# Gated tiles of an MLP split 70 places later, and per-token factors spread by two split-format matmuls

## The chip, the cores and the metric

The kernel runs on one core of a Trainium2 chip. A core has five engines, each with a queue of its own that it works through in order: TensorE (PE in the profile, matmuls; PEld is the loading of their weights), VectorE (DVE), ScalarE (ACT), GpSimd (POOL) and SyncE (SP, which here only issues DMAs). Engines wait for each other by semaphores. The metric is the device time of one execution in microseconds (us); less is better. Before the change it is 2059.86 us, the median of 3 runs (2059.63 to 2059.95).

## What is computed

One encoder layer on 512 tokens of 2048 channels in float32. Cut to the calls that matter:

```python
def rms_norm(x, g):
    xf = x.astype(jnp.float32)
    y = xf * lax.rsqrt(jnp.mean(xf * xf, axis=-1, keepdims=True) + EPS)
    return (y * g.astype(jnp.float32)).astype(x.dtype)
...
    xn = rms_norm(x, attn_norm_g[l])
    proj = jnp.einsum("bsd,dc->bsc", xn, w_in[l])
    u_val, u_gate, q, k, v = jnp.split(proj, split_pts, axis=-1)
    y_conv = conformer_conv(u_val, u_gate, ...)      # gate, conv of width 31, layer_norm, silu
    y_na = neighborhood_attention(heads(q), heads(k), heads(v), rpb[l])
    mixed = jnp.concatenate([rms_norm(y_conv, conv_out_g[l]), rms_norm(y_na, na_out_g[l])], axis=-1)
    x = x + jnp.einsum("bsc,cd->bsd", mixed, w_out[l])
    xn = rms_norm(x, ffn_norm_g[l])
    up = jnp.einsum("bsd,df->bsf", xn, w_up[l])
    up = depthwise_conv(up, ffn_dw_w[l], ffn_dw_b[l])      # width 3
    gate, val = jnp.split(up, 2, axis=-1)
    x = x + jnp.einsum("bsf,fd->bsd", jax.nn.silu(gate) * val, w_down[l])
return rms_norm(x, final_norm_g)
```

The inner width of the gated MLP is 5632, that is 44 tiles of 128 rows.

## The kernel before, in words

Channels lie on the 128 partitions and the 512 tokens along the free dimension, so a tile is 128x512. All large products are made from split operands: a float32 tile becomes a high part in the reduced matmul format (F32R) and a low part, the rest, in the same format. `parts` (lines 111 to 116) does this for weights: the high part `whi` by ACT, then the low part `wlo` by DVE, 128x1024 each. `mm3` (lines 122 to 127) then makes three matmuls of each pair: high by high, high by low, low by high. `whi` and `wlo` have four buffers each, the loaded weights (`raw`) seven; `weights` (lines 146 to 151) orders loads and splits three units ahead of their use.

The order of the work: the code is written as one stream, and a scheduler (the tile framework) hands each engine its instructions by a priority that counts up along the program. `shifted(by)` (lines 77 to 83) moves what stands inside it by so many places in that count. `tick` (lines 132 to 140) runs the next piece of a side job (statistics, attention) behind a matmul.

Per-token factors: a normalisation needs 1/sqrt of a mean over channels, which lie on partitions. `rsqrt_steps` (lines 170 to 198) sums squares by small matmuls with a matrix of ones, which leaves one value per token, tokens on partitions (128x4); computes the root and a Newton step on these; and then spreads the values over all 128 partitions and back onto the token axis: DVE multiplies the identity by each column of the values (`dg`, line 190, four 128x128 blocks), and one matmul with `ones` (`st`, line 193) adds up each column. With `keep`, ACT copies the result to SBUF (line 197); this is so at five uses (first norm, layer norm, both group norms, MLP norm). The last norm, in two halves, reads it from PSUM and has `keep=False`.

The MLP (lines 585 to 776) works in 11 chunks (c) of 4 inner tiles (i). For each inner tile, `up` (lines 638 to 699) makes gate and value with seven products instead of eight (a Strassen-like scheme: sums of weights `ws` and `raw` by DVE in `factors`, lines 585 to 611). A product is seven 512-column matmuls with `whi` (line 646), eight 256-column ones with `wlo` (line 651) and a last with `whi`. The first chunk uses `up_apart` with plain `mm3`. `hidden` (lines 738 to 745) scales by the MLP norm's factor, makes the width-3 convolution (`conv3`: one ACT step and two DVE steps each, the taps, lines 732 to 735), the silu (ACT, 743) and gate times value (DVE, 744). `in_two` (lines 747 to 751) splits the gated tile: `hh` by ACT (749), `hl` by DVE (750), and line 774 calls it for the four tiles at the end of a chunk. `down` (lines 753 to 765) multiplies the four split tiles of the chunk before by `w_down`, two output tiles (pd) per unit of weights: `mm3` over four tiles, a copy out of PSUM by ACT (764), and a DMA by POOL that adds it to the output in DRAM (765). Between the products of chunk c stand the down units of chunk c-1, at places 3 and 6 of the seven products (`down_units`, lines 616 to 623). The last chunk's down products come at the very end (`half`, lines 816 to 830), followed by the last norm.

Of the kernel before, what the change touches and what calls it, by code (L numbers as in the profile page):

```python
# [10 lines left out]
F32 = mybir.dt.float32  # L11
F32R = mybir.dt.float32r
AF = mybir.ActivationFunctionType
ALU = mybir.AluOpType
AX = mybir.AxisListType

P = 128
D = 2048
S = 512
# [47 lines left out]
def layer(ctx: ExitStack, tc: tile.TileContext, xT, w_in, w_out, w_up, w_down, par, tab, out):  # L67
    nc = tc.nc
    consts = ctx.enter_context(tc.tile_pool(name="consts", bufs=1))
    wpool = ctx.enter_context(tc.tile_pool(name="w", bufs=3))  # L70
    tp = ctx.enter_context(tc.tile_pool(name="t", bufs=NT))
    sm = ctx.enter_context(tc.tile_pool(name="sm", bufs=2))
    dram = ctx.enter_context(tc.tile_pool(name="dram", bufs=1, space=bass.MemoryType.DRAM))
    psm = ctx.enter_context(tc.tile_pool(name="psm", bufs=3, space=bass.MemoryType.PSUM))
    psa = ctx.enter_context(tc.tile_pool(name="psa", bufs=1, space=bass.MemoryType.PSUM))

    @contextmanager
    def shifted(by):

        at = tc.cur_priority  # L80
        tc.cur_priority = max(at + by, 0)
        yield
        tc.cur_priority = at + (tc.cur_priority - max(at + by, 0))

    def t2(name, dt=F32):
        return tp.tile([P, S], dt, tag="t2k", name=name)
# [12 lines left out]
        o = POFF[name] + i  # L99
        return prm[:, o:o + 1]  # L100

    ones = consts.tile([P, P], F32, name="ones")
    nc.vector.memset(ones, 1.0)
    ident = consts.tile([P, P], F32, name="ident")
    make_identity(nc, ident)
# [64 lines left out]
    def rsqrt_steps(accs, n, name, to=slice(0, S), keep=True):  # L170

        if not isinstance(accs, tuple):
            accs = accs,
        m = (to.stop - to.start) // P
        ps = psa.tile([P, 2, S], F32, tag="sc", name="st")[:, 0]
        for i in range(m):
            for acc in accs:
                nc.tensor.matmul(ps[:, i:i + 1], acc[:, to.start + i * P:to.start + (i + 1) * P], ones[:, 0:1],
                                 start=acc is accs[0], stop=acc is accs[-1])
        v, r, y = (sm.tile([P, S // P], F32, tag="rs" + c, name="rs" + c)[:, :m] for c in "vry")  # L180
        nc.vector.tensor_scalar(v, ps[:, :m], 1.0 / n, EPS, op0=ALU.mult, op1=ALU.add)
        nc.scalar.activation(r, v, AF.Sqrt)
        nc.vector.reciprocal(r, r)
        nc.vector.scalar_tensor_tensor(y, r, -0.5, r, op0=ALU.mult, op1=ALU.mult)
        nc.vector.tensor_mul(y, y, v)
        nc.vector.scalar_tensor_tensor(y, y, 1.5, r, op0=ALU.add, op1=ALU.mult)

        dg = t2("dg")
        for i in range(m):
            nc.vector.tensor_scalar(dg[:, i * P:(i + 1) * P], ident, y[:, i:i + 1], None, op0=ALU.mult)  # L190
        yield
        ps = psa.tile([P, 2, S], F32, tag="sc", name="st")[:, 0]
        nc.tensor.matmul(ps[:, :m * P], ones, dg[:, :m * P], start=True, stop=True)
        if not keep:
            return ps[:, :m * P]
        res = t2(name)
        nc.scalar.activation(res[:, to], ps[:, :m * P], AF.Copy)
        return res

    def rsqrt_value(g):  # L200
# [26 lines left out]
    ps = psa.tile([P, S], F32, tag="po", name="idle")  # L227
# [5 lines left out]
    for k in range(KD):  # L233
        x1.append(t2("x"))
        last = pin(nc.sync.dma_start(x1[k], xT[k]))
        h, l = t2("xh", F32R), t2("xl", F32R)
# [8 lines left out]
    for step in ORDER:  # L245
        i = next(a_ if step == "a" else q_)
# [9 lines left out]
    def stats1():  # L256
        for k in range(KD):
            sum_sq(acc1, x1[k], k == 0)
            if k % 4 == 3:
                yield  # L260
        for _ in range(STAT_AT):
            yield
        rstd.append((yield from rsqrt_steps(acc1, D, "rstd1")))
# [58 lines left out]
    def group_a():  # L322
        yield
        yield
        acc = t2("acc")
        nc.vector.tensor_add(acc, ys[0], ys[1])
        for i in range(2, NC_):
            nc.vector.tensor_add(acc, acc, ys[i])
        yield
        ps = psa.tile([P, 2, S], F32, tag="sc", name="st")[:, 0]  # L330
        nc.tensor.matmul(ps, ones, acc, start=True, stop=True)
        mu = t2("mu")
        nc.vector.tensor_scalar(mu, ps, 1.0 / CONV, None, op0=ALU.mult)
        acc = t2("acc")
        for i in range(NC_):
            nc.vector.tensor_sub(ys[i], ys[i], mu)
            sum_sq(acc, ys[i], i == 0)
        yield
        yield
        r = yield from rsqrt_steps(acc, CONV, "rln")  # L340
        acc = t2("acc")
        for i in range(NC_):
            nc.vector.tensor_mul(ys[i], ys[i], r)
            nc.scalar.activation(ys[i], ys[i], AF.Silu, scale=pc("lng", i), bias=pc("lnb", i))
            ma.append(split(ys[i], pc("cog", i), "ma"))
        for i in range(NC_):
            sum_sq(acc, ys[i], i == 0)
        for _ in range(RA_AFTER):
            yield

        ra.append((yield from rsqrt_steps(acc, CONV, "ra")))
# [123 lines left out]
    p, n = -1, 0  # L475
# [140 lines left out]
    def down_units(c, i, at):  # L616

        n = U // CH
        if not c:
            return ()  # L620
        if c < NCH - 1:
            return {3: (4 * i,), 6: (4 * i + n,)}.get(at, ())
        return {(1, 3): (0,), (1, 6): (2,), (2, 3): (4,), (2, 6): (6,), (3, 6): range(8, KD, n)}.get((i, at), ())
# [114 lines left out]
    def hidden(f, between):  # L738
        g, v = (up_apart if f < CH else up)(f, between)
        nc.vector.tensor_mul(g, g, rstd2[0])  # L740
        nc.vector.tensor_mul(v, v, rstd2[0])
        g, v = conv3(g, f), conv3(v, NF + f)
        nc.scalar.activation(g, g, AF.Silu)
        nc.vector.tensor_mul(g, g, v)
        return g

    def in_two(g):
        h, l = t2("hh", F32R), t2("hl", F32R)
        nc.scalar.activation(h, g, AF.Copy)
        nc.vector.tensor_sub(l, g, h.bitcast(F32))  # L750
        return h, l

    def down(hs, ds, wide=False):

        for d0 in ds:
            w = weights()
            for d in range(d0, d0 + U // CH):

                ps = (psm.tile([P, S], F32, tag="mm", name="pd") if wide and d % 5 > 1 else
                      psa.tile([P, S], F32, tag="tr", name="pd", bufs=2))  # L760
                for k in range(CH):
                    mm3(ps, w, (d - d0) * CH + k, *hs[k], k == 0, k == CH - 1)
                t = t2("pdc")
                nc.scalar.activation(t, ps, AF.Copy)  # L764
                nc.gpsimd.dma_start(xd[d], t, accum_op=ALU.add)  # L765

    pend = None
    for c in range(NCH):
        hs = []
        for i in range(CH):  # L770

            last = c == NCH - 1 and i == CH - 1
            hs.append(hidden(c * CH + i, lambda at: None if last else down(pend, down_units(c, i, at))))
        hs = [in_two(h) for h in hs]
        if not last:
            pend = hs

# [140 lines left out]
```

## Time and profile before

| | before |
|---|---|
| median of 3 runs | 2059.86 us |
| the profiled execution | 2060.74 us |
| its span | 2059.0 us |
| granted TensorE clock, mean | 0.997 |
| DMA, mean | 134 GB/s |

The span is the time from the first to the last instruction on the chip; the execution has 1.7 us around it. In the rows below, a line such as `L750 DVE TENSOR_TENSOR hl<-uy,hh 128x512` is line 750 of the kernel on DVE, writing tile hl from uy and hh. A timeline row begins with its start and its length in us; `x7` at its end means seven instructions merged into it, and a bracket tells how long the engine stood idle before it and what released it. Matmuls overlap: their cost is the distance from start to start, not their length. In a stretch row, busy times of the engines stand in the order PE, PEld, DVE, ACT, POOL, each with a count, and then the granted clock, the DMA share and GB/s.

### The profile page before, as it was taken

To read this page: it belongs to the slowest core of one execution; us is meant where nothing else is said; L and a number is where in the kernel's file an instruction comes from. 1 tells how busy PE (TensorE), PEld (TensorE's weight loads), DVE (VectorE), ACT (ScalarE), POOL (GpSimd) and SP (SyncE) were. 2 spreads that over 40 slices of the span, in tenths; PEclk is the share of its full clock that TensorE was granted. 3 is DMA by queue.
4 is the path that set the end of the run, shared out by engine and by line. 5 is a ranking of instruction groups with operands and counts; after the bars stand their busy time and mean duration, and the time that the engine had idled before them with its cause. 6 is when DMAs were issued, how large, how long until landed. Compare 5 with 4: busy or idle time off the path is not lost.

```text
span 2059.0 us, 28552 instructions
## 1 busy us (share of the span) xinstructions
PE 2038.8 (99%) x10810; PEld 1734.1 (84%) x10810; DVE 1665.1 (81%) x2316; ACT 1065.3 (52%) x1728; POOL 156.3 (8%) x186
## 2 busy tenths in 40 slices
PE   9999999999999999999999999999999999999997
PEld 7887888787788998888888888888888888888887
DVE  7986697687567898888888878878888888889876
ACT  6244424447436545555555555555554554555562
POOL 0000000000001001111111111111111111110110
PEclk9999999999999999999999999999999999999998
DMA  7323232335436535656566565565565566564682
GB/s 252 107 90 101 72 123 82 111 95 175 149 106 170 147 113 129 138 145 134 131 150 138 125 148 143 128 144 143 132 135 143 125 145 144 134 138 124 147 211 82
DMA packets 99113, 275.38 MB, mean 134 GB/s; under 512 B 10912, under 2 KB 15520, under 8 KB 98976
## 3 DMA queue, kind: packets, MB, share of 16 engines
q1 hardware_dynamic: 73616, 227.40, 36.6%
q0 software_dynamic: 25216, 46.15, 15.6%
q8 instruction: 85, 1.39, 0.3%
q14 instruction: 52, 0.43, 0.1%
q10 hardware_dynamic: 144, 0.01, 0.0%
HBM read 218.99 MB, written 54.53 MB: 133 GB/s over the span
## 4 chain that ended last, share of the span: by engine, by line
PE 93%; DVE 3%; DMA 1%; issue 1%; ACT 1%; SPq 0%; DVEq 0%; ACTq 0%
PE pu L646 23%; PE pu L651 12%; PE pd L127 8%; PE pd L125 8%; PE pd L126 8%; PE pj L125 7%; PE pj L126 7%; PE pj L127 7%; PE po L125 3%; PE po L126 3%; PE po L127 3%; PE pu L125 1%; PE pu L127 1%; PE pu L126 1%; DVE hl L750 1%
## 5 line engine op out<-in xcount | busy, mean ns | idle before, releaser
L115 DVE TENSOR_TENSOR wlo<-raw,whi 128x1024 fp32r<-128x1024 f32 x364 | 444.3, 1221 | 247.1 <-ACT whi L114 225.8
L114 ACT ACTIVATE whi<-raw 128x1024 fp32r<-128x1024 f32 x364 | 384.4, 1058 | 469.1 <-PE pj L126 175.3
L646 PE MATMUL pu<-xc,whi 128*128 128x512 f32 x2240 | 573.5, 392 | 0.3 <-ACT pl L658 0.3
L646 PEld LDWEIGHTS pu<-xc,whi 128*128 128x128 f32 x2240 | 408.6, 189 | 74.1 <-ACT pl L658 0.7
L651 PEld LDWEIGHTS pu<-xc,wlo 128*128 128x128 f32 x2240 | 305.6, 190 | 21.8
L651 PE MATMUL pu<-xc,wlo 128*128 128x256 f32 x2240 | 312.3, 282 | 0.0
L125 PE MATMUL pj<-xh,whi 128*128 128x512 f32 x640 | 252.4, 398 | 0.9 <-DVE gate L301 0.5
L127 PE MATMUL pd<-hh,wlo 128*128 128x512 f32 x640 | 249.1, 391 | 2.2 <-DVE wlo L115 2.2
L126 PE MATMUL pj<-xl,whi 128*128 128x512 f32 x640 | 250.2, 391 | 0.1
L125 PE MATMUL pd<-hh,whi 128*128 128x512 f32 x640 | 250.0, 391 | 0.0
L127 PE MATMUL pj<-xh,wlo 128*128 128x512 f32 x640 | 249.8, 390 | 0.0
L126 PE MATMUL pd<-hl,whi 128*128 128x512 f32 x640 | 249.1, 389 | 0.0
L765 POOL DMA_DIRECT2D x2d<-pdc x160 | 139.3, 872 | 1168.1 <-ACT pdc L764 1065.0
L658 ACT ACTIVATE pl<-pu 128x256 f32<-128x256 f32 x280 | 105.1, 380 | 173.4 <-PE pu L646 173.4
L316 DVE SCALAR_TENSOR_TENSOR y<-ch,prm,y 128x508 f32<-128x508 f32 (+14 forms) x240 | 173.1, 741 | 4.1
L114 ACT ACTIVATE whi<-ws 128x1024 fp32r<-128x1024 f32 x132 | 139.7, 1058 | 68.0 <-PE pu L646 43.5
L115 DVE TENSOR_TENSOR wlo<-ws,whi 128x1024 fp32r<-128x1024 f32 x132 | 160.9, 1219 | 1.3 <-ACT whi L114 1.2
L125 PEld LDWEIGHTS pj<-xh,whi 128*128 128x128 f32 x640 | 120.0, 188 | 32.3 <-issue 3.7
L127 PEld LDWEIGHTS pd<-hh,wlo 128*128 128x128 f32 x640 | 120.2, 188 | 30.9 <-DVE wlo L115 5.7
L764 ACT ACTIVATE pdc<-pd 128x512 f32<-128x512 f32 x160 | 93.9, 588 | 95.9 <-PE pd L127 95.9
L126 PEld LDWEIGHTS pj<-xl,whi 128*128 128x128 f32 x640 | 120.3, 188 | 26.0 <-DVE xl L238 1.8
L126 PEld LDWEIGHTS pd<-hl,whi 128*128 128x128 f32 x640 | 120.2, 188 | 25.6
(172 smaller groups left out, 2775.0 us busy)
## 6 DMA issues: line engine op xcount, KB each, us to landing
raw<-in_w_up SPq DMA_DIRECT2D x176, 512.0 KB, 3.7
raw<-in_w_down SPq DMA_DIRECT2D x88, 512.0 KB, 4.0
x2d<-pdc POOLq DMA_DIRECT2D x160, 256.0 KB, 4.8
raw<-in_w_in SPq DMA_DIRECT2D x76, 512.0 KB, 3.9
raw<-in_w_out SPq DMA_DIRECT2D x32, 512.0 KB, 3.8
x<-in_xT SPq DMA_DIRECT2D x32, 256.0 KB, 5.5
tab<-in_tab SPq DMA_DIRECT2D x32, 256.0 KB, 4.5
x2d<-x SPq DMA_DIRECT2D x16, 256.0 KB, 2.2
```

The costliest lines, as they stand in the source:

```text
L114: i = nc.scalar.activation(hi[:, :n], raw[:, :n], AF.Copy)
L115: j = nc.vector.tensor_sub(lo[:, :n], raw[:, :n], hi[:, :n].bitcast(F32))
L125: nc.tensor.matmul(ps, hi[:, a], mh, start=start, stop=False)
L126: nc.tensor.matmul(ps, hi[:, a], ml, start=False, stop=False)
L127: return nc.tensor.matmul(ps, lo[:, a], mh, start=False, stop=stop)
L316: nc.vector.scalar_tensor_tensor(y[:, a:b], h[:, a + j - PAD:b + j - PAD], prm[:, o + j:o + j + 1], y[:, a:b], op0=ALU.mult, op1=ALU.add)
L646: return nc.tensor.matmul(ps, w[0][:, k * P:(k + 1) * P], comb[c][k], start=k == 0, stop=k == U - 1)
L651: nc.tensor.matmul(ps[:, H:], w[1][:, k * P:(k + 1) * P], comb[c][k][:, :H], start=False, stop=False)
L658: nc.scalar.activation(to, ps, AF.Copy)
L750: nc.vector.tensor_sub(l, g, h.bitcast(F32))
L764: nc.scalar.activation(t, ps, AF.Copy)
L765: nc.gpsimd.dma_start(xd[d], t, accum_op=ALU.add)
```

## The change

Two edits. At the end of each chunk of the MLP but the last, the split of the four gated tiles is put 70 places further down the program's order. And where `rsqrt_steps` keeps its result, the per-token values are split into a high and a low part, two 128x512 diagonal tiles in the split format are made by one DVE product each (identity and values both spread by a stride of zero), and two accumulating matmuls in that format take the place of one in full precision. The matrix of ones becomes an F32R tile, read as float32 elsewhere.

```diff
-    ones = consts.tile([P, P], F32, name="ones")
+    ones_r = consts.tile([P, P], F32R, name="ones")
+    ones = ones_r.bitcast(F32)
...
-        dg = t2("dg")
-        for i in range(m):
-            nc.vector.tensor_scalar(dg[:, i * P:(i + 1) * P], ident, y[:, i:i + 1], None, op0=ALU.mult)
+        if not keep:
+            dg = t2("dg")
+            for i in range(m):
+                nc.vector.tensor_scalar(dg[:, i * P:(i + 1) * P], ident, y[:, i:i + 1], None, op0=ALU.mult)
+            yield
+            ps = psa.tile([P, 2, S], F32, tag="sc", name="st")[:, 0]
+            nc.tensor.matmul(ps[:, :m * P], ones, dg[:, :m * P], start=True, stop=True)
+            return ps[:, :m * P]
+
+        yh = sm.tile([P, S // P], F32R, tag="rsh", name="rsh")
+        nc.vector.tensor_copy(yh, y)
+        nc.vector.tensor_sub(y, y, yh.bitcast(F32))
+        ds = []
+        for part in (yh.bitcast(F32), y):
+            ds.append(t2("dg", F32R))
+            nc.vector.tensor_mul(ds[-1].rearrange("p (i k) -> p i k", k=P), ident.unsqueeze(1).broadcast_to([P, m, P]),
+                                 part.unsqueeze(2).broadcast_to([P, m, P]))
         yield
         ps = psa.tile([P, 2, S], F32, tag="sc", name="st")[:, 0]
-        nc.tensor.matmul(ps[:, :m * P], ones, dg[:, :m * P], start=True, stop=True)
-        if not keep:
-            return ps[:, :m * P]
+        for i, dg in enumerate(ds):
+            nc.tensor.matmul(ps, ones_r, dg, start=i == 0, stop=i == 1)
         res = t2(name)
-        nc.scalar.activation(res[:, to], ps[:, :m * P], AF.Copy)
+        nc.scalar.activation(res, ps, AF.Copy)
         return res
...
-        hs = [in_two(h) for h in hs]
+        with shifted(0 if last else 70):
+            hs = [in_two(h) for h in hs]
         if not last:
             pend = hs
```

## Prediction

> **What bounds the kernel now.** I read the page's busy line and its chain first, then the stretches, then the waits of TensorE (PE), then the timelines of PE and VectorE (DVE) where the changed code runs.
>
> ```profile
> PE 2038.8 (99%) x10810; PEld 1734.1 (84%) x10810; DVE 1665.1 (81%) x2316; ACT 1065.3 (52%) x1728; POOL 156.3 (8%) x186
> PE 93%; DVE 3%; DMA 1%; issue 1%; ACT 1%; SPq 0%; DVEq 0%; ACTq 0%
> ```
>
> PE is busy 99% of the span and is 93% of the chain that ended last. So a change can gain only by fewer PE cycles or by the few pauses of PE that are left, and it loses whatever new pause it puts into PE's queue. Four stretches (the columns are time, PE, PEld, DVE, ACT and POOL busy, then PE's granted clock):
>
> ```profile
> 520.00:580.00 60.00, 58.95 (x311) 47.31 (x312) 35.21 (x58) 28.54 (x53) 0.00 (x0) 1.00 0.36 114
> 700.00:720.00 20.00, 20.00 (x164) 19.52 (x163) 19.12 (x32) 10.51 (x14) 0.00 (x0) 1.00 0.34 104
> 960.00:1120.00 160.00, 159.73 (x845) 137.48 (x844) 133.74 (x169) 87.25 (x136) 17.42 (x20) 1.00 0.60 136
> 2045.00:2059.00 14.00, 1.27 (x3) 0.50 (x2) 6.08 (x19) 0.59 (x2) 2.78 (x4) 0.53 0.45 150
> ```
>
> In the MLP (third row) PE is covered and DVE has 16% left. The one wait there is in the list of waits (us in total, times, longest), and PE's timeline shows it in place, at the end of a chunk, where the products with the next chunk's weights meet the first down products of the last chunk:
>
> ```profile
> PE pd L127 <- DVE wlo L115: 2.2, 8, 0.3
> ```
> ```profile
> 903.08 0.40 PE L125 MATMUL pd<-hh,whi 128*128 128x512 f32 x1
> ...
> 903.77 0.40 PE L126 MATMUL pd<-hl,whi 128*128 128x512 f32 x1
> 904.44 0.50 PE L127 MATMUL pd<-hh,wlo 128*128 128x512 f32 x1 [0.27 <-DVE wlo L115]
> 904.78 0.40 PE L125 MATMUL pd<-hh,whi 128*128 128x512 f32 x1
> ...
> 905.24 1.75 PE L646 MATMUL pu<-xc,whi 128*128 128x512 f32 x7
> 906.83 1.11 PE L651 MATMUL pu<-xc,wlo 128*128 128x256 f32 x8
> ```
>
> Start to start a 512-column matmul takes 0.23 us (903.08 to 903.77 are three). From 903.77 to 904.44 are 0.67, and to 904.78 another 0.34: 0.44 of wait and 0.11 to get going again, 0.55 us, eight times by the waits. One more end of a chunk has its pause elsewhere:
>
> ```profile
> 1881.26 0.39 PE L646 MATMUL pu<-xc,whi 128*128 128x512 f32 x1
> 1882.00 1.88 PE L646 MATMUL pu<-xc,whi 128*128 128x512 f32 x7 [0.34 <-ACT pl L658]
> 1883.72 1.11 PE L651 MATMUL pu<-xc,wlo 128*128 128x256 f32 x8
> ```
>
> 0.74 instead of 0.23, then seven in 1.72 instead of 1.59 (905.24 to 906.83): 0.64. All ten ends of chunks now cost 8 x 0.55 + 0.64 = 5.0 us.
>
> **Part 1, the later split of the gated tiles.** The diff sets lines 774 to 775 (hh on ScalarE, ACT; hl on DVE) 70 places later in priority. The listing of the two built programs shows what comes of it. SP's and POOL's queues keep their order to the last DMA; DVE's, ACT's and PE's change at the ends of chunks. DVE's queue here, changed kernel below (its lines stand 1 to 14 higher), names shortened to the tiles:
>
> ```
> before: wlo, tap, ws add, tap, tap, hl0, tap, hl1, g*v, hl2, wlo(down), hl3, wlo, vv add, wlo, ws add
> after:  wlo, tap, ws add, tap, tap, wlo(down), tap, wlo, g*v, hl0, ws add, wlo, hl1, raw add, hl2, hl3, vv add
> PE before: hh0 hl0 hh0' hl0' wlo0 hh1 hl1 | next product | the rest
> PE after:  hh0 hh0' hl0 wlo0 hl0' hh1 wlo0' hh1' hl1 wlo1 hh2 hl1' wlo1' hh2' hl2 wlo2 hh3 | next product
> ```
>
> (hl0 in PE's rows is the matmul that reads hl0; a dash marks the second output tile.) So the weight split for which PE waits moves ahead of hl, and hl moves behind two weight splits; hl1 and hl2 go behind two more 1024-column steps and a third. PE's queue, in order, still meets hl0 third, before the next product that could fill the time. Durations are in DVE's timeline:
>
> ```profile
> 895.78 1.23 DVE L115 TENSOR_TENSOR wlo<-raw,whi 128x1024 fp32r<-128x1024 f32 x1 [2.13 <-ACT whi L114]
> 896.97 0.75 DVE L733 SCALAR_TENSOR_TENSOR uy<-g,prm,uy 128x511 f32<-128x511 f32 x1
> 897.64 1.22 DVE L596 TENSOR_TENSOR ws<-raw 128x1024 f32<-128x1024 f32 x1
> 898.77 0.75 DVE L734 SCALAR_TENSOR_TENSOR uy<-g,prm,uy 128x511 f32<-128x511 f32 x1
> 899.43 0.75 DVE L733 SCALAR_TENSOR_TENSOR uy<-vl,fwn,uy 128x511 f32<-128x511 f32 x1
> 900.10 0.69 DVE L750 TENSOR_TENSOR hl<-uy,hh 128x512 fp32r<-128x512 f32 x1
> ...
> 903.17 1.22 DVE L115 TENSOR_TENSOR wlo<-raw,whi 128x1024 fp32r<-128x1024 f32 x1
> 904.30 0.68 DVE L750 TENSOR_TENSOR hl<-uy,hh 128x512 fp32r<-128x512 f32 x1
> 904.90 1.22 DVE L115 TENSOR_TENSOR wlo<-ws,whi 128x1024 fp32r<-128x1024 f32 x1
> 906.04 0.68 DVE L673 TENSOR_TENSOR vv<-vv,pl 128x512 f32<-128x512 f32 x1
> ```
> ```profile
> 894.69 1.06 ACT L114 ACTIVATE whi<-raw 128x1024 fp32r<-128x1024 f32 x1 [1.90 <-PE pd L126]
> ...
> 897.55 0.62 ACT L749 ACTIVATE hh<-uy 128x512 fp32r<-128x512 f32 x1
> 898.07 1.05 ACT L114 ACTIVATE whi<-raw 128x1024 fp32r<-128x1024 f32 x1
> ...
> 900.67 1.05 ACT L114 ACTIVATE whi<-ws 128x1024 fp32r<-128x1024 f32 x1
> ...
> 903.28 1.06 ACT L114 ACTIVATE whi<-raw 128x1024 fp32r<-128x1024 f32 x1
> ```
>
> Queued back to back, DVE steps follow at 1.13 us (1024 columns), 0.66 (a tap) and 0.60 (512 columns), and a 512-column result is there 0.69 after its step starts; PE starts 0.05 after DVE ends (904.39 to 904.44). DVE's run starts at 895.78 in both kernels, because its high half waits (first ACT row) until PE releases a weight buffer. This ties DVE to PE, so the lateness does not wear off from chunk to chunk. From 900.10 in the new order: wlo and tap to 901.89; the second wlo (its high half is done at 901.72) to 903.02; g*v to 903.62; hl0 ends at 904.31. PE, which reached the down products at 903.08 and did two matmuls, wants it at 903.54 and gets it at 904.36: **wait 0.82**.
>
> Next on DVE: ws add at 904.22, wlo at 905.35 (its high half, the fourth ACT row, is done at 904.34), hl1 at 906.48, ended 907.17. From hl0 to hl1 PE has six matmuls: 904.36 + 1.38 = 905.74, and it starts at 907.22: **wait 1.48**. Then raw add at 907.08, hl2 at 908.21, ended 908.90, PE at 908.95 against 907.22 + 1.38 = 908.60: **wait 0.35**. hl3 has the next product in front of it and costs nothing. On ACT hh1 stands behind that fourth row and ends near 904.9 (0.62, the hh row); PE reaches it three matmuls after hl0, at 905.05, so ACT stays hidden by 0.1 to 0.2.
>
> SP's weight loads wait for DVE to have read a buffer, so they slip with DVE:
>
> ```profile
> raw<-in_w_up SPq DMA_DIRECT2D x176, 512.0 KB, 3.7
> ```
>
> A load lands after 3.7 us and the splits of DVE wait for ACT's high half and PE's buffers, not for it; I charge nothing, and up to 0.3 per end of a chunk if that cover is gone.
>
> The waits give 2.65, and three new starts at 0.11 make it 3.0 us. I take this at all ten ends of chunks: 10 x 3.0 = 30.0, less the 5.0 that is paid now, since the wait for wlo goes: **+25.0 us**. The first and the last have other neighbours in the listing; I put no more precision into them. Bounds: without the 0.11s, 26.5 - 5.0 = 21.5; with 0.1 more on each of the thirty waits, 28.0.
>
> **Part 2, factors in split format.** Five of the seven uses keep their result and change. One full-precision matmul goes, two split-format ones come.
>
> ```profile
> 574.53 1.02 PE L193 MATMUL st<-dg,ones 128*128 128x512 f32 x2
> 574.99 0.79 PE L125 MATMUL po<-mah,whi 128*128 128x512 f32 x1
> 575.62 0.39 PE L126 MATMUL po<-mal,whi 128*128 128x512 f32 x1
> ```
> ```profile
> 571.13 0.16 DVE L185 TENSOR_TENSOR rsy<-rsy,rsv 128x4 f32<-128x4 f32 x1
> 571.33 0.17 DVE L186 SCALAR_TENSOR_TENSOR rsy<-rsy,rsr 128x4 f32<-128x4 f32 x1
> 571.53 0.88 DVE L190 TENSOR_SCALAR dg<-ident,rsy 128x128 f32<-128x128 f32 x4
> 572.31 0.69 DVE L521 TENSOR_TENSOR oa<-po,ra 128x512 f32<-128x512 f32 x1
> ```
>
> From 574.53 to 575.62 are 1.09, of which the matmul of L125 is 0.23: 0.86 for the factor. Two of the split format take 0.46: 0.40 saved, five times 2.0. On DVE the four diagonal blocks take 0.78 (571.53 to 572.31). The new ones are two small steps of 0.20 (571.13 to 571.33) and two 128x512 products. No row shows a product with both operands spread; I bound one by a 1024-column step, 1.13, and by two of the old blocks, 0.39, and take hl's 0.60, whose size and output format are the same: 1.6, 0.8 more per use. PE meets the second matmul some matmuls after the first, so most of this is hidden by them. The fifth use (700 to 720, DVE busy 19.12 of 20) has no slack on DVE: of its 0.8 I charge 0.4 (bounds 0 and 0.8). Sum **-1.6 us** (bounds -2.0, and +2 with spread products at 1.13 each, 1.1 more per use, of which 0.8 is seen).
>
> **Sum.** 25.0 - 1.6 = +23.4. The profiled execution took 2060.74 (span 2059.0), 0.88 above the median of three; the difference goes onto the median: 2059.86 + 23.4 = **2083.3 us**.
>
> **Rivals.**
> *The wait goes and none comes* (faster). The weight split is ahead of hl now, and if hl0 still ends by 903.54 the 5.0 are gained: 2059.9 - 5.0 - 1.6 = 2053.3. It decides at 0.82 us: a DVE run that starts that much earlier than 895.78. For it: 2.13 us of idle DVE ahead of that row. Against: the same row says that the idle time ended with whi, and ACT's that whi waited for PE. Chance 0.04.
> *Only hl0 is late* (no difference). If the steps between hl0 and hl2 got done in PE's time, ten waits of 0.82 + 0.11 stand against 5.0 and 1.6: +2.7, 2062.6. Against: 1.13 + 1.13 + 0.60 is more than the 1.38 of six matmuls. Chance 0.06.
> *The clock falls as well* (slower still). The last stretch shows PE at 0.53 of its clock once it mostly waits, while 520 to 580, with 1.05 us without PE, kept 1.00. The new pauses sum to 2.65 within some 5.4 us. If each end of a chunk ran its next seven wide matmuls (905.24 to 906.83) at half clock, 1.6 us more, that is +16: 2099. Against: 520 to 580, and no single pause is above 1.5. Chance 0.06.
> The Trainium skill, "TensorE: Matmul & The Clock Gate", section "A second HAM failure mode: psum-queue depth-cycling", says that frequent short pauses between groups of matmuls can make the clock swing down and up; its section "What's actually happening" wants a whole idle window of about 3.4 us before the clock halves. By the first of them the third rival comes true, by the second the clock stays up; the row 520 to 580 agrees with the second, and no run here shows the first.
> That the shift does nothing is out: the queues listed above differ.
>
> **How the numbers follow.** The forecast has 0.84 and the range 2076 to 2090, which leaves out the rivals, 0.16 together. Its low end is Part 1 at +18 (no 0.11s, each wait 0.1 shorter) and Part 2 at -2.0: +16. Its high end is Part 1 at its bound of +28 and Part 2 at its bound of +2: +30. A measurement of this kernel tells about 0.2% (4 us) from no change. Faster 0.04 (the first rival), same 0.06 (the second), slower 0.90 (the forecast and the third).
>
> **What would show it.** In the changed profile PE's waits should name hl (line 764) at each end of a chunk, about 0.8, 1.5 and 0.35 us long, and no wlo; PE's idle time grows by 20 us or more, DVE's busy time by about 4; PEclk stays at 9s; the factor's matmuls show as pairs 0.23 apart. It is wrong if hl's waits are missing, if DVE runs its wlo before 895.78's equivalent, or if a clock below 1.0 stands in an MLP stretch.

## The result, and the profile after

The changed kernel takes **2083.92 us** (median of 5 runs, 2082.29 to 2087.02) against 2059.95 for the kernel before on the same chip (5 runs, 2059.63 to 2064.78): 1.0112 times as long, 95% interval 1.01 to 1.0124. The forecast was 2083.3, with a range of 2076 to 2090. Its profiled execution took 2085.22, its span is 2083.4, 24.4 more than before.

The page's busy line, its chain of work and the first rows of PE's waits (us in total, times, longest), after:

```profile
PE 2044.3 (98%) x10810; PEld 1735.3 (83%) x10810; DVE 1667.2 (80%) x2316; ACT 1063.6 (51%) x1728; POOL 156.5 (8%) x186
PE 89%; DVE 5%; issue 2%; DMA 2%; ACT 1%; POOL 0%; SPq 0%; DVEq 0%; POOLq 0%; ACTq 0%
```
```profile
PE pd L127 <- DVE hl L764: 18.1, 17, 2.9
PE pu L660 <- ACT whi L115: 2.3, 1, 2.3
```

PE has the same number of instructions and DVE 2.1 us more of work (1665.1 to 1667.2), but PE has idle time that was not there: the span grew by 24.4 and PE's busy time by 5.5. The list of waits names hl, line 764, as the place; wlo is gone from it. The second row is a new one that the prediction doesn't have. PE's timeline at the second end of a chunk, after (before, at 903.08, it had one pause of 0.44 there):

```profile
906.16 0.62 PE L126 MATMUL pd<-hh,whi 128*128 128x512 f32 x2
907.46 0.50 PE L127 MATMUL pd<-hl,whi 128*128 128x512 f32 x1 [0.67 <-DVE hl L764]
907.79 0.40 PE L128 MATMUL pd<-hh,wlo 128*128 128x512 f32 x1
...
908.72 0.39 PE L126 MATMUL pd<-hh,whi 128*128 128x512 f32 x1
910.33 0.50 PE L127 MATMUL pd<-hl,whi 128*128 128x512 f32 x1 [1.22 <-DVE hl L764]
...
911.59 0.40 PE L126 MATMUL pd<-hh,whi 128*128 128x512 f32 x1
912.07 0.50 PE L127 MATMUL pd<-hl,whi 128*128 128x512 f32 x1
```

Read it by starts, not by brackets: 0.23 from start to start is free running. Two hh matmuls start at 906.16 and 906.39, the hl one was due at 906.62 and starts at 907.46: 0.83 with the digits that the rows round off. 908.72 to 910.33 is 1.38 too long, 911.59 to 912.07 is 0.25 too long. Behind each pause the next distance is 0.34, 0.11 over. Together 2.78 us, the same at all eight inner ends to 0.01. DVE's timeline for the same end, after:

```profile
898.87 1.23 DVE L116 TENSOR_TENSOR wlo<-raw,whi 128x1024 fp32r<-128x1024 f32 x1 [2.13 <-ACT whi L115]
...
903.18 1.22 DVE L116 TENSOR_TENSOR wlo<-raw,whi 128x1024 fp32r<-128x1024 f32 x1
...
904.98 1.22 DVE L116 TENSOR_TENSOR wlo<-ws,whi 128x1024 fp32r<-128x1024 f32 x1
...
906.71 0.69 DVE L764 TENSOR_TENSOR hl<-uy,hh 128x512 fp32r<-128x512 f32 x1
907.31 1.22 DVE L621 TENSOR_TENSOR ws<-ws,raw 128x1024 f32<-128x1024 f32 x1
908.45 1.23 DVE L116 TENSOR_TENSOR wlo<-raw,whi 128x1024 fp32r<-128x1024 f32 x1
909.58 0.69 DVE L764 TENSOR_TENSOR hl<-uy,hh 128x512 fp32r<-128x512 f32 x1
910.18 1.23 DVE L612 TENSOR_TENSOR raw<-raw 128x1024 f32<-128x1024 f32 x1
911.32 1.30 DVE L764 TENSOR_TENSOR hl<-uy,hh 128x512 fp32r<-128x512 f32 x2
```

It is the queue of the prediction, step by step: two wlo ahead of the first hl, a sum of weights and a third wlo ahead of the second. The bracket of the first row is still 2.13, as before: DVE's run starts when PE lets go of a weight buffer, so DVE never gets ahead. It is not short of time, at 80% of the span; it is late all the same.

The first end of a chunk looks otherwise. PE's timeline there, after, and the stretches around it (time, busy of PE, PEld, DVE, ACT and POOL, granted clock, DMA share, GB/s):

```profile
779.75 0.62 PE L126 MATMUL pd<-hh,whi 128*128 128x512 f32 x2
783.33 0.79 PE L127 MATMUL pd<-hl,whi 128*128 128x512 f32 x1 [2.95 <-DVE hl L764]
783.92 0.63 PE L128 MATMUL pd<-hh,wlo 128*128 128x512 f32 x1
784.35 0.63 PE L126 MATMUL pd<-hh,whi 128*128 128x512 f32 x1
```
```profile
783.00:786.40 3.40, 3.07 (x7) 2.48 (x8) 3.40 (x5) 1.86 (x6) 0.00 (x0) 0.51 0.00 0
905.00:915.00 10.00, 8.03 (x39) 5.90 (x38) 8.22 (x11) 3.98 (x9) 0.00 (x0) 1.00 0.34 105
1905.00:1908.50 3.50, 3.13 (x10) 2.56 (x11) 3.50 (x6) 2.72 (x8) 0.00 (x0) 0.65 0.78 208
```

One pause of 3.11 us, and then matmuls 0.43 apart instead of 0.23 for about 3 us: the granted clock is 0.51 (first stretch). At an inner end, with 2.46 us of waits in three pieces, it stays at 1.00 (second stretch). What decides between the two is told in the last section. The last end, at 1902.72, has a pause of 2.42, the second row of the waits, and then the low clock too (third stretch). What ACT waits for there, in its timeline of the same profile:

```profile
1904.26 1.06 ACT L115 ACTIVATE whi<-ws 128x1024 fp32r<-128x1024 f32 x1 [2.31 <-DVE ws L621]
```

In all, over the free-running distances: 4.65 at the first end, 8 x 2.78, and 4.04 at the last. Before they were 0, 8 x 0.54 and 0.61. With PE 1.60 earlier at the first end (779.75 against 781.35) the sum is -1.6 + 4.65 + 8 x 2.24 + 3.43 = **24.4**, all of the 24.4.

### The profile page after: what moved, and what is told of

It reads as the page before. It is cut to its first block, busy times and chain, and to the rows that moved or that the text cites. A ratio compares the mean times of both kernels' runs of the same rounds, so it can differ in the third digit from the quotient of the medians.

```text
span 2083.4 us, 28559 instructions
## 1 busy us (share of the span) xinstructions
PE 2044.3 (98%) x10810; PEld 1735.3 (83%) x10810; DVE 1667.2 (80%) x2316; ACT 1063.6 (51%) x1728; POOL 156.5 (8%) x186
## 4 chain that ended last, share of the span: by engine, by line
PE 89%; DVE 5%; issue 2%; DMA 2%; ACT 1%; POOL 0%; SPq 0%; DVEq 0%; POOLq 0%; ACTq 0%
PE pu L660 22%; PE pu L665 11%; PE pd L127 7%; PE pd L128 7%; PE pd L126 7%; PE pj L126 7%; PE pj L127 7%; PE pj L128 7%; PE po L126 2%; PE po L127 2%; PE po L128 2%; DVE wlo L116 1%; PE pu L126 1%; PE pu L128 1%; PE pu L127 1%
## 5 line engine op out<-in xcount | busy, mean ns | idle before, releaser
L330 DVE SCALAR_TENSOR_TENSOR y<-ch,prm,y 128x501 f32<-128x501 f32 (+14 forms) x240 | 173.3, 743 | 4.2
L128 PEld LDWEIGHTS pj<-xh,wlo 128*128 128x128 f32 x640 | 120.2, 188 | 25.8 <-DVE wlo L236 0.8
```

The costliest lines, as they stand in the source:

```text
L128: return nc.tensor.matmul(ps, lo[:, a], mh, start=False, stop=stop)
L330: nc.vector.scalar_tensor_tensor(y[:, a:b], h[:, a + j - PAD:b + j - PAD], prm[:, o + j:o + j + 1], y[:, a:b], op0=ALU.mult, op1=ALU.add)
```

## The experiments

Theory: the time is the sum of what PE waits for hl at the ten ends, by DVE's queue; the factors give a little back. Rivals: that some of it is a lower clock, and that the factors aren't a gain. All excess times below are worked out as above, from start to start in PE's timeline of the profiled execution, pauses, restarts and slow matmuls together.

| kernel | median us (runs) | ratio to before, 95% interval | first end | each inner end | last end |
|---|---|---|---|---|---|
| before | | | 0 | 0.54 | 0.61 |
| changed | 2083.92 (5) | 1.0112, 1.01 to 1.0124 | 4.65 | 2.78 | 4.04 |
| e1 factors only | 2060.87 (11) | 1.0001, 0.9992 to 1.001 | 1.95 | 0.54 | 0.58 |
| e2 shift only | 2084.09 (4) | 1.011, 1.0096 to 1.0124 | 1.85 | 2.77 | 4.33 |
| e3 shift at inner ends | 2079.27 (4) | 1.0088, 1.0074 to 1.0102 | 2.06 | 2.77 | 0.62 |
| e4 shift of 25 | 2057.83 (11) | 0.9984, 0.9975 to 0.9993 | 1.38 | 0.18 | 0.70 |
| e5 shift of 100 | 2102.68 (4) | 1.0206, 1.019 to 1.0221 | 6.48 | 4.55 | 4.15 |
| e6 shift of -30 | 2057.87 (11) | 0.9986, 0.9978 to 0.9995 | 0.98 | 0.18 | 1.26 |
| e7 hl on GpSimd | 2107.15 (4) | 1.0227, 1.0213 to 1.0241 | 6.22 | 3.9 to 6.6 | 6.27 |
| e8 shift of 28, old factors | 2057.30 (11) | 0.9983, 0.9974 to 0.9992 | 0 | 0.07 | 0.22 |
| e9 four factors | 2058.94 (10) | 0.9993, 0.9984 to 1.0002 | | | |
| e10 four factors, shift of 28 | **2055.08** (9) | 0.9975, 0.9965 to 0.9985 | 0 | 0.08 | 0.70 |
| e11 shift of 60 | 2077.36 (4) | 1.0078, 1.0064 to 1.0092 | 6.09 | 1.63 | 4.97 |
| e12 four factors again | 2059.12 (8) | 0.9995, 0.9984 to 1.0007 | 0 | 0.54 | 0.72 |

The edits are against the changed kernel unless another is named. The kernel before took 2060.6 to 2060.9 beside these runs.

**e1, the factors alone.**

```diff
-        with shifted(0 if last else 70):
+        with shifted(0):
```


> The split of the gated tiles stays where it was; only the factors are spread by two split-format matmuls. Theory (waits for hl carry the loss, the factor edit saves PE cycles): 2058 to 2059 us, 1 to 2 us below before; no wait for hl, the waits for wlo at the ends of chunks as before. Rival (the longer VectorE work of the spread products carries part of the loss): 2063 us or more, with pauses of TensorE near 47, 466, 511, 573 or 707 us.

2060.87 against 2060.9: no difference, so the saving was missed. It is made and lost again. PE's timeline of e1 at the first end, and DVE's ahead of it:

```profile
779.31 0.62 PE L126 MATMUL pd<-hh,whi 128*128 128x512 f32 x2
781.41 0.50 PE L127 MATMUL pd<-hl,whi 128*128 128x512 f32 x1 [1.48 <-DVE hl L764]
```
```profile
773.29 0.69 DVE L754 TENSOR_TENSOR g<-g,rstd 128x512 f32<-128x512 f32 x1
775.75 1.23 DVE L610 TENSOR_TENSOR ws<-raw 128x1024 f32<-128x1024 f32 x1 [1.78 <-DMA raw<-in_w_up]
...
778.03 0.75 DVE L747 SCALAR_TENSOR_TENSOR uy<-g,prm,uy 128x511 f32<-128x511 f32 x1
```

PE comes to its down products at 779.31, two us earlier than before (781.35). But on DVE a sum of weights now stands between the scaling (L754) and the taps (L747), and it waits 1.78 us for a load. Taps and hl queue behind it; PE waits 1.64. From 903.76 on PE is where it was before (903.77).

**e2, the shift alone.** Before's kernel with the shift of 70 (the last fence of the diff above, the old `rsqrt_steps`).

> Only the split of the gated tiles moves by 70 places; the factors keep their one full-precision matmul. Theory: 2083 to 2086 us, before plus 23 to 26, with the three waits for hl of 0.8, 1.4 and 0.25 us at the ends of chunks. Rival (the edits need each other): clearly below 2080.

2084.09, and 23.2 over before, as expected; the changed kernel is 24.0 over before. So the shift is nearly all of the change, and the rival is out. The 0.8 us between the two are less than the intervals tell apart (2.5 to 3 us either way). But no gain of the factors is left beside the shift either, and the traces show where it goes: with them the first end costs 4.65 instead of 1.85.

**e3, the shift at the eight inner ends alone.**

```diff
-        with shifted(0 if last else 70):
+        with shifted(70 if 0 < c < NCH - 2 else 0):
```


> Both edits, but the shift by 70 at the eight inner ends of chunks alone; the first and the last end keep the old order. Theory (in the changed kernel the first and the last end cost more than the others, because their pauses of 3.1 and 2.4 us are followed by matmuls 0.43 us apart, at half clock): 8 x 2.2 us of net waits, less 1 to 2 of the factor edit: 2076 us, and no 512-column matmul slower than 0.24 us apart after 700 us except right after a wait. Rival (all ten ends cost the same): 2079 us.

The median is 2079.27 (2078.0 to 2081.42): by the number this is the rival's 2079 and not the theory's 2076, so the traces have to tell the two apart. The theory had counted on 1 to 2 us of the factors, which e1 doesn't have. The trace gives 8 x 2.23 = 17.8 for the inner ends over e1's time of 2060.87, which is 2078.7, and no more; its own execution is the one of 2078.0. PE's timeline of e3 at one end, and the stretch around it:

```profile
1028.17 0.50 PE L127 MATMUL pd<-hl,whi 128*128 128x512 f32 x1 [0.67 <-DVE hl L764]
...
1031.04 0.51 PE L127 MATMUL pd<-hl,whi 128*128 128x512 f32 x1 [1.21 <-DVE hl L764]
```
```profile
960.00:1120.00 160.00, 158.03 (x829) 135.29 (x829) 131.41 (x166) 87.19 (x137) 17.89 (x21) 1.00 0.57 134
```

So the inner ends are waits at full clock. The ten ends don't all cost the same: without the shift the last one costs 0.62 instead of 4.04 and the first 2.06 instead of 4.65, and no clock below 1.00 is left at either. The low clock belongs to the two outer ends.

**e4, e5, e6 and e11: other shifts**, 25, 100, -30 and 60 in the place of 70.

> Both edits, with a shift of 25 places in place of 70. In the built queue hl0, hl1 and hl2 stay ahead, and the down weights' wlo goes ahead of the last hl alone. Theory (what counts is how many 1024-column steps of VectorE stand between PE and hl): the 0.55 us waits for wlo at the eight inner ends go and no wait for hl comes: 2053 to 2056 us, below before and below e1. Rival (any later split costs): above e1.

> Both edits, shift of 100 places. In the built queue hl0 stands behind more 1024-column steps still, so that TensorE should pause once for about 3.1 us at each inner end (worked from VectorE's spacings of 1.13 and 0.60 us). Theory on the waits alone: about 3.1 + 0.35 us per end, 2091 us. With the rule seen at the first end of the changed kernel (a pause of 3.1 us is followed by matmuls 0.43 us apart for about 1.5 us): 1 to 2 us more at each end, 2100 to 2110 us. Rival (the loss comes from the order of TensorE's own queue, not from how late hl is): about as the changed kernel, 2084.

> Both edits, but the split of the gated tiles put 30 places ahead of its old place. In the built queue hl0 to hl2 then stand before the down weights' wlo with less between. Theory (lateness of what TensorE meets next on VectorE): the 0.55 us waits at the inner ends go, no wait for hl: 2056 to 2059 us, near the shift of 25. Rival (only a later place frees the wlo): as before or above, 2061.

> Kernel: the changed kernel with 60 places in place of 70. Theory (the time goes by where hl stands in DVE's queue, not by the number of places; with 60 one 1024-column step fewer stands ahead of hl1, so the second wait falls from 1.4 to about 0.4): pauses of 0.8, 0.4 and 0.3 us at the inner ends with 0.11 each, about 1.8 in place of 2.78, so some 8 to 10 us less than the changed kernel: 2074 to 2077. Rival (any place beyond the covered one costs the same): 2083 to 2085.

With 25 and with -30 the inner ends cost 0.18 and the kernel is faster than before, by 3.1 and 2.8 us, which is little (0.15%), but both intervals lie below 1. For e4 more was expected: the inner ends do give 8 x 0.36 = 2.9, but of the first end's 1.95 in e1 1.38 stays, and 2060.87 - 2.9 - 0.6 is 2057.4. With 60 the second wait is 0.24 instead of 1.38, as expected, since a step of 1024 columns fewer stands ahead of hl1; that saves 8 x 1.15 = 9.2 us, but longer pauses at the first and last end (3.37 and 3.30) take 2.4 of it back, and it comes out just above the expected range. Why these two are longer with 60 than with 70 was not followed up. With 100 each inner end has one pause of 3.10 and then the low clock (the first end has 4.91, the last 2.53). PE's timeline and a stretch of e5, and a single pause elsewhere in e4 with the stretch behind it:

```profile
1038.24 0.79 PE L127 MATMUL pd<-hl,whi 128*128 128x512 f32 x1 [2.94 <-DVE hl L764]
1038.83 0.63 PE L128 MATMUL pd<-hh,wlo 128*128 128x512 f32 x1
1039.26 0.63 PE L126 MATMUL pd<-hh,whi 128*128 128x512 f32 x1
```
```profile
1037.50:1041.00 3.50, 2.76 (x7) 2.18 (x8) 3.50 (x6) 1.36 (x5) 0.00 (x0) 0.55 0.54 150
```
```profile
694.93 0.39 PE L126 MATMUL pu<-xc,whi 128*128 128x256 f32 x1 [2.04 <-ACT xc L549]
```
```profile
695.00:698.00 3.00, 3.00 (x15) 3.00 (x16) 2.65 (x8) 3.00 (x9) 0.00 (x0) 0.53 0.62 152
```

In e5 an inner end costs 4.55: 3.10 of wait, and 1.45 of slow restart and slow matmuls. With the clock the time is where the theory had it. None of the four rivals came true. The time doesn't go by the number of places alone: -30 and 25 both gain, 60 costs 17 us and 100 costs 42. What counts is which steps of DVE stand ahead of hl.

**e7, hl on GpSimd**, to take the late work off DVE.

```diff
-        nc.vector.tensor_sub(l, g, h.bitcast(F32))
+        nc.gpsimd.tensor_sub(l, g, h.bitcast(F32))
```


> The changed kernel with its shift of 70, but hl is subtracted by GpSimd in place of VectorE, so no 1024-column step can stand in front of it. Theory (VectorE's queue makes hl late): the waits of 0.8, 1.4 and 0.25 us go; the last hl, which needs gate times value, is some 1.3 us late at each end: 2065 to 2072 us. Rival (TensorE's changed order, or hh on ScalarE, costs the time): 2080 us or more.

2107.15, far from what the theory expected and, by the number, on the rival's side. The waits of PE, and DVE and POOL at one end (timelines of e7):

```profile
PE pd L126 <- ACT hh L763: 12.9, 9, 2.4
PE pd L127 <- POOL hl L764: 10.2, 10, 1.1
PE pd L128 <- DVE wlo L116: 6.0, 7, 0.9
```
```profile
1413.36 1.79 DVE L748 SCALAR_TENSOR_TENSOR uy<-g,prm,uy 128x511 f32<-128x511 f32 x1
...
1416.78 2.31 DVE L116 TENSOR_TENSOR wlo<-raw,whi 128x1024 fp32r<-128x1024 f32 x1
```
```profile
1412.89 3.42 POOL L764 TENSOR_TENSOR hl<-uy,hh 128x512 fp32r<-128x512 f32 x2 [0.79 <-ACT hh L763]
```

At this end three of the four hl are in time (at 1417.67 PE starts the hh matmul and at 1417.90, with no wait, the hl one), and only the last is waited for, 1.09. But the DVE steps that start beside POOL's take 1.79 instead of 0.75 and 2.31 instead of 1.22. All of DVE's queue is later, with it wlo, the last gated tile, its hh and its hl. So the first row of the waits, for hh, doesn't speak for the rival: ACT starts the last hh at 1421.52, after 2.60 us of waiting for gate times value on DVE. What e7 was to show, that it is DVE's queue that makes hl late, it shows for three of the four tiles, and nothing for the time.

**e8, e9, e12 and e10: the parts that gain.** e8 is before's kernel with a shift of 28. e9 and e12 have no shift, and the old full-precision factor at the MLP norm only; e10 is this with the shift of 28.

```diff
-        if not keep:
+        if not keep or name == "rstd2":
             dg = t2("dg")
...
-            return ps[:, :m * P]
+            if not keep:
+                return ps[:, :m * P]
+            res = t2(name)
+            nc.scalar.activation(res, ps, AF.Copy)
+            return res
```


> The shift alone, of 28 places, with the old full-precision factor matmul. Theory: the eight waits of 0.55 us go and the first end has no wait for hl, which e1 and e4 have there with the new factors: 2056 to 2058 us, at or below e4. Rival (the new factors save what they promise): above e4 by 1.6.

> Kernel: no shift; the split-format factor at the first norm, layer norm and both group norms, the old full-precision one at the MLP norm. Theory (the MLP norm's two longer DVE steps push the taps back at the first end of a chunk, where e1's PE waited 1.5 us for hl): with the old factor there that wait stays away and what four factors save, 4 x 0.40 = 1.6 us at most, is kept: 2058.4 to 2059.8. Rival (the first end's wait comes from PE being earlier there, whatever the factor): the wait stays and the time is e1's, 2060.9.

> Kernel: e9's once more, for a look at the first end of a chunk. Theory (the old factor at the MLP norm leaves DVE's queue there as it was): PE has no wait for hl at the first end, near 780 us, the other ends cost what they cost before the change, and the time is 2058.4 to 2059.8. Rival (the wait comes from PE being earlier there): a wait of 1.0 to 1.5 us for hl near 780, and e9's gain comes from somewhere else.

> Kernel: split-format factor at four uses as in e9, and the gated tiles' split 28 places later at the first ten ends of chunks. Theory (both savings add: e8's -2.6 us from the shift and e9's -1.0 to -1.6): 2055 to 2057, at or below e8. Rival (a pause elsewhere, as e4 had at 692, takes the factors' part back): 2057.3, e8's time.

e8 came out as expected, 2057.30: no wait at its first end, and 0.07 at the inner ones. e9's one traced execution took 5249.77 us, isn't read and isn't in the table; e12 is the same kernel with a trace. PE's timeline of e12 at the first end, and DVE's ahead of it:

```profile
779.55 0.40 PE L126 MATMUL pd<-hh,whi 128*128 128x512 f32 x1
779.79 0.39 PE L127 MATMUL pd<-hl,whi 128*128 128x512 f32 x1
```
```profile
772.50 1.22 DVE L116 TENSOR_TENSOR wlo<-raw,whi 128x1024 fp32r<-128x1024 f32 x1
773.64 0.74 DVE L751 SCALAR_TENSOR_TENSOR uy<-g,prm,uy 128x511 f32<-128x511 f32 x1
```

No pause, although PE is there 1.8 us earlier than before, and the taps follow a wlo without a load in between. So the wait of e1 comes from the order that the fifth factor brings about, not from PE's being early. e12 keeps the 1.8 us to the end in its trace (span 2057.0 against 2059.0); by the medians of e9 and e12 1.5 to 1.8, within 0.2%, and both intervals reach 1. In e10 the two gains add, as far as medians tell: 5.7 against 3.4 (e8) and 1.5 to 1.8, where the intervals of e8 and e10 overlap. PE's timeline at the second end, and the MLP stretch, of e10:

```profile
904.09 0.46 PE L127 MATMUL pd<-hl,whi 128*128 128x512 f32 x1
904.38 0.40 PE L128 MATMUL pd<-hh,wlo 128*128 128x512 f32 x1
```
```profile
960.00:1120.00 160.00, 160.00 (x843) 137.69 (x842) 134.00 (x168) 86.94 (x136) 17.48 (x20) 1.00 0.58 136
```

One distance of 0.29 is all that is left of the pauses at this end: on DVE the down products' weight split now starts ahead of hl1 (899.83 and 901.57) and the next one ahead of hl2, and each hl still ends before PE comes to it. e10 takes **2055.08**, 0.9975 of the time before: the fastest of the versions run, with four of the five factors.

## Why the prediction came true

The mechanism was right, PE waits for hl because DVE's queue is late, and it carries most of the time. The sum was 0.6 us off (23.4 forecast, 24.0 by the medians, 24.4 by the traces), and that close is luck, for its parts are not all as good.

- **What bounds it, the queues, the tie of DVE to PE**: right. DVE's rows after are the forecast ones in order, its run still starts behind the 2.13 us for whi, and the excess is the same at eight ends.
- **The three waits**: forecast 0.82, 1.48 and 0.35, found 0.83, 1.38 and 0.25, with 0.11 behind each: 2.78 instead of 3.0 per inner end, 1.8 us less for eight.
- **"I take this at all ten ends"**: the weak step. The outer ends were known to have other neighbours and were still counted like the rest. In e2 the first is 1.85 and the last 4.33 instead of 3.0: 1.2 less and 1.3 more. These and the inner ends give 25.0 - 1.8 - 1.2 + 1.3 = 23.3 for Part 1, and e2 measured 23.2 over before.
- **"PEclk stays at 9s"**: right on the page, whose slices are 52 us long, and wrong in the trace: "a clock below 1.0 in an MLP stretch" stands at both outer ends, 0.51 and 0.65. So the third rival did occur, at two of ten ends, and with it a sign that the prediction itself had named as proof against it. The rival had half clock after several short pauses; here it came after single long ones, while the inner ends, which it spoke of, kept 1.00. "No single pause is above 1.5" was wrong for the outer ends, and it is no reason for the inner ones: in e7 single pauses of 1.37 and less were enough (last section). The inner ends kept their clock because their 2.46 us are spread; of the two 3.41-us windows that hold them at 906 to 912, the emptier has PE busy for 2.37.
- **The last end**: its wait isn't for hl. There the next product comes first, and its high half waits behind ACT for a sum of weights (ws, L621) that DVE now makes after two wlo. The prediction looked for no such wait, and named hl for each end.
- **Part 2**: the saving exists (PE comes to the first end 1.60 earlier, and 2.04 in e1, for 2.0 in the sum), and the factor's matmuls stand 0.23 apart as forecast. The spread products follow at 0.60, the value that was chosen between 0.39 and 1.13. The wrong step is the cost of the fifth use: 0.4 for two longer DVE steps. These cost next to nothing themselves; the order of DVE's queue behind them changed, and a step that waits for a load got ahead of the taps. That cost 1.95 in e1, and in the changed kernel 2.8 more than in e2. I charged nothing for loads, "up to 0.3 per end of a chunk if that cover is gone"; it was gone at the first end, for 1.5 to 1.8 us.
- **The signs**: PE's idle time grew by 18.9, not "by 20 us or more", for the slow matmuls count as busy; DVE's busy time by 2.1, not "by about 4".

So Part 1 came out at +23.2 instead of +25.0 and Part 2, beside it, at +0.8 instead of -1.6: misses of -1.8 and +2.4 that nearly take each other away by luck. These are differences of medians. The trace of the changed kernel by itself shows such a trade too: 1.8 less at the inner ends, 1.6 and 1.0 more at the first and the last (4.65 and 4.04 instead of 3.0).

The Trainium skill, "TensorE: Matmul & The Clock Gate", has two rules that the prediction set against each other. Its section "What's actually happening" (a whole idle window of about 3.4 us before the clock halves) agrees with the inner ends, which kept 1.00, but a pause of 2.20 us was enough in e4, and 2.42 after; here the measurement decides. For the other section, "A second HAM failure mode: psum-queue depth-cycling", e7 shows something now: three short pauses, none above 1.38, with which the clock fell at some ends (last section).

## What to carry to other kernels

Where an engine is tied to the bound engine by a buffer, a step that is put later in its queue costs the time of all that goes ahead of it, again at every turn; write out both queues up to the next wait and add. Do this for the first and last turn by themselves, for the order there differs, one long wait can cost more than three short ones, and a step that waits for a load may have come to stand in front. A small saving early on is worth only what the next waiting place lets through, so follow it to the end before it enters the sum.

## What the runs showed of the hardware

**What decides the clock.** Single pauses of up to 1.84 us (first end in e3) left the clock at full speed. Pauses of 2.20 (e4), 2.38 and 2.58 (e7), 2.42 (after), 2.53 (e5), 2.69 (e2) and of 3.1 and more came with some 3 us of matmuls at 0.43 us per 512 columns instead of 0.23, or 0.21 instead of 0.12 per 256. But the single pause isn't what decides. In e7 the inner ends from 1163 on have the same three pauses, 1.01, 1.34 and 1.37 within 6 us, and three of these six ends fell to a low clock, three did not.

The record of the granted clock in the traces shows more. Within each trace it changes only at whole multiples of 3.41 us from its first change (the end of the trace aside), and each of the 23 low stretches between 690 and 1960 us, in thirteen traces (all but e9's), lasts 3.41 or 6.83 us. So one can cut a trace into windows of 3.41 us by this grid. Here are two windows in a row at each of two ends of chunks of e7, the first pair from one that fell (the first busy time is PE's, the clock stands third from the end):

```profile
1166.59:1170.01 3.42, 1.15 (x5) 0.67 (x4) 3.42 (x3) 2.00 (x6) 1.46 (x1) 1.00 0.26 101
1170.01:1173.42 3.41, 3.41 (x12) 2.82 (x11) 2.19 (x3) 0.00 (x0) 0.00 (x0) 0.50 0.54 153
1419.18:1422.59 3.41, 2.23 (x8) 1.38 (x8) 3.41 (x5) 1.07 (x4) 0.31 (x1) 1.00 0.46 154
1422.59:1426.00 3.41, 2.32 (x12) 1.86 (x12) 3.41 (x4) 0.93 (x4) 1.16 (x1) 1.00 0.14 17
```

At the first end two of the pauses lie in one window, PE is busy for 1.15 us of it, and the next window has half the clock. At the second the grid divides the same pauses between two windows, with 2.23 and 2.32, and the clock stays at 1.00. It is so in all thirteen traces between 690 and 1960 us: of the windows at full clock, the 23 with PE busy for 1.55 us or less were all followed by one at 0.50, and none of the 4774 with 1.73 or more was. The limit lies between, near half of the window. Among the small matmuls of the last norm, behind 2000 us, it is less clear: windows with 2.07 (e8) and 2.26 (e7) were followed by a low one there. All this is read off the traces; no run was made to test it.

The Trainium skill, "TensorE: Matmul & The Clock Gate", section "What's actually happening", has a free-running window for the clock, one that doesn't start anew with the kernel. The traces agree, and show that such a window need not be idle as a whole.

**DVE beside GpSimd.** In e7 a 512-column subtraction took 1.29 to 2.34 us on GpSimd, 0.69 on DVE, and the taps and weight splits of DVE, with two inputs from SBUF, that started while it ran took 1.0 to 1.1 us longer each; steps that had started before it did not. The Trainium skill, "GPSIMD Engine Reference", section "Specifications", states that GpSimd shares its SBUF interfaces with VectorE and that DVE steps with two SBUF inputs contend for them; e7 gives the price of that here.
